# First head pair's q, k, v and the gates projected together while x arrives, from ten larger SyncE transfers

## Chip, cores and metric

The kernel runs on one core of a Trainium2 chip. The metric is device time of one execution in microseconds (us). A run gives one time per execution; one further execution is profiled, and the profile's views all come from that one.

## What is computed

Two decoder layers on x of 512 positions and width 1024, batch 1, all in fp32. Layer 0 mixes positions by forgetting attention with 16 heads, layer 1 by a gated linear recurrence; behind each mixer stands a gated MLP with a causal convolution. The part around the change is the head of layer 0:

```
h = rmsnorm(x, att_norm_g)
proj = h @ w_in                       # 1024 -> 3*1024 + 16
q, k, v, fl = split(proj, [D, 2*D, 3*D])
logf = log_sigmoid(fl + b_f)
c = cumsum(logf, axis=1)
logits = q k^T / 8 + (c_t - c_s), causal
o = softmax(logits) v ; x = x + o @ w_out
```

## The kernel before

Everything is kept transposed: the 1024 features lie on 8 blocks of 128 partitions, the 512 positions on the free axis, so that x is eight blocks of 128x512. TensorE (PE) multiplies fp32 numbers in two parts. `split` (lines 66 to 68) makes of a tile a rounded part (`..h`, a cast on ScalarE, line 67) and the rest (`..l`, a subtraction on VectorE, line 68), and `mm3` (lines 81 to 84) sums three products: weight h by x h (L82), weight h by x l (L83), weight l by x h (L84). One block of 128 outputs from 1024 inputs is therefore 24 matmuls of 128x512 in one PSUM bank.

The gain of the norm is put on x first (`Norm.block`, lines 175 to 183: `xh` on ScalarE at L180, `xl` on VectorE at L181); the factor 1/rms needs all of x, so it is applied behind the projections. `Norm.square` (lines 185 to 193) sums the squares (`nsq` on ScalarE, `nacc` on VectorE), and `Norm.finish` (lines 195 to 208) sums over partitions with a plain fp32 matmul (`nss`, L199) and makes `rstd` of it.

The start stands at lines 231 to 269. SyncE (SP) issues the gains, x block 0, and then weights and x in pieces (`pieces`, line 238): x blocks 0, 1 to 3, 4 to 7, each piece led by its part of the q and the k weights of head pair 0 (`wst`, tiles of 64, 192 and 256 KB). Per block of x, six matmuls go into the banks of q and k (`pj_q0`, `pj_k0`). Behind them come the norm, the v weights of head pair 0 as one 512 KB transfer (line 265, `pj_v0`, 24 matmuls), and the forget gates (lines 266 to 269, `pj_wf`: 24 matmuls with only 16 output rows). The attention section (lines 303 to 509) then runs as four generators that take turns: `projections` (q, k, v of the other seven head pairs, each by a 512 KB transfer through `chunk` into one of two `raw` tiles), `operands` (`qk`, `forget`, `values`: scaling by `rstd`, and for q and k small SP copies into the tiles QX, QQ, KX, KK), `maxima` (row maxima `mxp`) and `attend` (`lg`, `pv`). Results stay in `oh`, `ol` of `opool`, whose buffers x and the first weights used before.

The text gives what depends on what; the order in which each engine's instructions stand is set when the program is built, by the framework's scheduler, engine by engine, and each engine then runs its list in that order. A transposition `vT` (L351) of the v of head pair 0 is the first PE instruction that needs `rstd`.

## Time and profile before

| | us |
|---|---|
| median of 3 runs | 1275.23 (1274.2 to 1275.55) |
| profiled execution, its own time | 1275.21 |
| its span | 1273.5 |
| PE busy | 1252.6 (98%) |
| DVE busy (VectorE) | 802.7 (63%) |
| ACT busy (ScalarE) | 589.7 (46%) |
| POOL busy (GpSimd) | 44.7 (4%) |
| the chain that ended last, share of PE | 94% |

The span is the time from the first to the last instruction in the profile; the execution's own time is 1.7 us more. PE's matmuls are pipelined: a matmul's duration in a row (0.39 us) is longer than the distance from its start to the next one's start (0.23 us), so times of a row of matmuls are read from their starts. PEld is the load of the next stationary operand.

### The profile page before, as it was taken

To read this page: it belongs to the slowest core of one execution; us is meant where nothing else is said; L and a number is where in the kernel's file an instruction comes from. 1 tells how busy PE (TensorE), PEld (TensorE's weight loads), DVE (VectorE), ACT (ScalarE), POOL (GpSimd) and SP (SyncE) were. 2 spreads that over 40 slices of the span, in tenths; PEclk is the share of its full clock that TensorE was granted. 3 is DMA by queue.
4 is the path that set the end of the run, shared out by engine and by line. 5 is a ranking of instruction groups with operands and counts; after the bars stand their busy time and mean duration, and the time that the engine had idled before them with its cause. 6 is when DMAs were issued, how large, how long until landed. Compare 5 with 4: busy or idle time off the path is not lost.

```text
span 1273.5 us, 15653 instructions
## 1 busy us (share of the span) xinstructions
PE 1252.6 (98%) x5994; PEld 1039.3 (82%) x5994; DVE 802.7 (63%) x1227; ACT 589.7 (46%) x827; POOL 44.7 (4%) x120
## 2 busy tenths in 40 slices
PE   7999999999999999999999999999999999999997
PEld 5778888888888888888888988987888888888886
DVE  6767767387777777333367585566777777762233
ACT  6355556464444444222266565554544444442231
POOL 2011110000000000000010000000000000000001
PEclk9999999999999999999999999999999999999998
DMA  6544554233333333333322222222233332333321
GB/s 197 149 128 108 134 134 124 89 127 99 100 100 99 98 91 91 91 98 98 95 85 82 81 70 83 84 67 92 91 100 99 100 98 90 96 90 93 96 85 66
DMA packets 43307, 127.25 MB, mean 100 GB/s; under 512 B 5617, under 2 KB 8305, under 8 KB 43233
## 3 DMA queue, kind: packets, MB, share of 16 engines
q1 hardware_dynamic: 42592, 125.56, 32.9%
q8 instruction: 47, 0.77, 0.3%
q10 hardware_dynamic: 544, 0.52, 0.1%
q14 instruction: 28, 0.22, 0.1%
q0 software_dynamic: 96, 0.18, 0.1%
HBM read 111.43 MB, written 2.10 MB: 89 GB/s over the span
## 4 chain that ended last, share of the span: by engine, by line
PE 94%; DVE 2%; ACT 2%; DMA 1%; issue 0%; SPq 0%; POOL 0%; DVEq 0%; ACTq 0%
PE pj_up L84 13%; PE pj_up L82 13%; PE pj_up L83 13%; PE pj_dn L82 6%; PE pj_dn L84 6%; PE pj_dn L83 6%; PE i L634 1%; PE i L633 1%; PE i L631 1%; PE pj_who L83 1%; PE pj_who L84 1%; PE pj_who L82 1%; PE pj_hf L82 1%; PE pj_hf L83 1%; PE pj_hf L84 1%; PE pj_hg L84 1%
## 5 line engine op out<-in xcount | busy, mean ns | idle before, releaser
L82 PE MATMUL pj_up<-xh_f,wh_up 128*128 128x512 f32 x704 | 273.9, 389 | 0.0
L83 PE MATMUL pj_up<-xl_f,wh_up 128*128 128x512 f32 x704 | 273.9, 389 | 0.0
L84 PE MATMUL pj_up<-xh_f,wl_up 128*128 128x512 f32 x704 | 273.9, 389 | 0.0
L83 PEld LDWEIGHTS pj_up<-xl_f,wh_up 128*128 128x128 f32 x704 | 132.2, 188 | 27.6
L84 PEld LDWEIGHTS pj_up<-xh_f,wl_up 128*128 128x128 f32 x704 | 132.2, 188 | 27.4
L82 PEld LDWEIGHTS pj_up<-xh_f,wh_up 128*128 128x128 f32 x704 | 132.2, 188 | 27.3
L82 PE MATMUL pj_dn<-gh,wh_dn 128*128 128x512 f32 x330 | 130.8, 396 | 0.0
L83 PE MATMUL pj_dn<-gl,wh_dn 128*128 128x512 f32 x330 | 130.8, 396 | 0.0
L84 PE MATMUL pj_dn<-gh,wl_dn 128*128 128x512 f32 x330 | 130.8, 396 | 0.0
L67 ACT CAST wh_up<-raw_up 128x1024 fp32r<-128x1024 f32 x88 | 92.7, 1054 | 65.9 <-PE pj_up L83 50.6
L68 DVE TENSOR_TENSOR wl_up<-raw_up,wh_up 128x1024 fp32r<-128x1024 f32 x88 | 107.9, 1226 | 15.4 <-ACT wh_up L67 11.9
L68 DVE TENSOR_TENSOR wl_dn<-raw_dn,wh_dn 128x1024 fp32r<-128x1024 f32 (+1 forms) x45 | 51.1, 1136 | 98.2 <-ACT wh_dn L67 97.9
L543 DVE TENSOR_TENSOR us<-pj_up,rstd_f 128x512 f32<-128x512 f32 x88 | 60.6, 688 | 78.4 <-PE pj_up L84 78.2
L67 ACT CAST wh_dn<-raw_dn 128x1024 fp32r<-128x1024 f32 (+1 forms) x45 | 44.1, 980 | 140.4 <-PE pj_dn L83 109.1
L67 ACT CAST gh<-y 128x512 fp32r<-128x512 f32 x44 | 27.3, 621 | 115.5 <-DVE y L551 115.5
L546 ACT ACTIVATE y<-us,cv 128x512 f32<-128x512 f32 x88 | 71.7, 815 | 8.5 <-DVE us L543 7.3
L84 PEld LDWEIGHTS pj_dn<-gh,wl_dn 128*128 128x128 f32 x330 | 62.2, 188 | 15.2
L83 PEld LDWEIGHTS pj_dn<-gl,wh_dn 128*128 128x128 f32 x330 | 62.2, 188 | 15.2
L82 PEld LDWEIGHTS pj_dn<-gh,wh_dn 128*128 128x128 f32 x330 | 62.1, 188 | 15.1
L548 DVE SCALAR_TENSOR_TENSOR y<-us,cv,y 128x512 f32<-128x512 f32 x88 | 66.2, 752 | 3.0
L547 DVE SCALAR_TENSOR_TENSOR y<-us,cv,y 128x512 f32<-128x512 f32 x88 | 65.7, 746 | 0.2
L550 ACT ACTIVATE y<-y 128x512 f32<-128x512 f32 x44 | 27.8, 632 | 79.5 <-DVE y L548 79.5
(369 smaller groups left out, 2379.3 us busy)
## 6 DMA issues: line engine op xcount, KB each, us to landing
raw_up<-in_wup SPq DMA_DIRECT2D x88, 512.0 KB
raw_dn<-in_wdn SPq DMA_DIRECT2D x30, 512.0 KB
raw_dn<-in_wdn SPq DMA_DIRECT2D x15, 384.0 KB
raw_v<-in_wqkv SPq DMA_DIRECT2D x8, 512.0 KB
raw_wo<-in_wo SPq DMA_DIRECT2D x8, 512.0 KB
raw_hf<-in_wh SPq DMA_DIRECT2D x8, 512.0 KB
raw_hq<-in_wh SPq DMA_DIRECT2D x8, 512.0 KB
raw_hg<-in_wh SPq DMA_DIRECT2D x8, 512.0 KB
```

The costliest lines, as they stand in the source:

```text
L67: A.copy(dst_h, src)
L68: V.tensor_tensor(dst_l, src, dst_h.bitcast(F32), op=ALU.subtract)
L82: PE.matmul(o, wh_, xh_, start=first, stop=False)
L83: PE.matmul(o, wh_, xl_, start=False, stop=False)
L84: PE.matmul(o, wl_, xh_, start=False, stop=last)
L543: V.tensor_mul(u[:, 2:], o, rstd)
L546: A.activation(y, u[:, 2:], AF.Identity, scale=k(2), bias=k(3))
L547: V.scalar_tensor_tensor(y, u[:, 1:S + 1], k(1), y, op0=ALU.mult, op1=ALU.add)
L548: V.scalar_tensor_tensor(y, u[:, 0:S], k(0), y, op0=ALU.mult, op1=ALU.add)
L550: A.activation(ys[0], ys[0], AF.Silu)
L631: PE.matmul(o, xh[kk][:, ts_], hs, start=kk == 0 and i % 2 == 0, stop=False, skip_group_check=True)
L633: PE.matmul(o, xh[kk][:, ts_], ls, start=False, stop=False, skip_group_check=True)
```

## The change

SP loads the start in ten transfers (five of x, five of weights): x blocks 0 and 1 singly, then in pairs, and from a new input `wqkv0`, in which the host has put the q, k and v weights of head pair 0 side by side by block of x, block 0 singly, blocks 1 and 2, 3 and 4, 5 and 6 in pairs, block 7 singly. The gains go out on ScalarE's queue and the gates' weights on GpSimd's. Eight matmuls on a constant tile (`warm`) stand ahead of everything on PE. Per block of x, nine matmuls go into the banks of q, k and v; the gates' weights lie in one tile `fw` of 48 columns per block (h part in columns 0 to 15, l part in 32 to 47, zeros between), so that two matmuls per block, 16 in place of 24, give both parts, which `forget` adds (one ScalarE copy and one VectorE addition more). The squares are interleaved with the blocks, and `nss` comes behind the gates. `oh` and `ol` become four tiles of two blocks each. Line numbers of the changed kernel from here on are higher than before by 3 to 17 (`split` is still L67 and L68, `mm3` is L85 to L87, `xl` is L184, `nacc` L196, the gates' matmuls L261 and L262).

```diff
@@ -228,45 +231,54 @@
         def tmp(name, rows=P):
             return ap_.tile([rows, S], F32, tag="tmp", name=name, bufs=3)
+        norm = Norm(G_ATT, "a")
+        warm = side("warm")
+        for i in range(8):
+            PE.matmul(warm[:, :P], ones, ones, start=True, stop=True)
+        xin = [opool.tile([P, 2, S], F32, name=f"xin{j}", bufs=1, tag=f"oh{j}") for j in range(NT)]
+        fraw = ap_.tile([P, NB, HEADS], F32, name="fraw", tag="tmp", bufs=3)
+        nc.scalar.dma_start(gn, gains)
+        nc.gpsimd.dma_start(fraw, wf)
+        wst = []
+        for i, (wa, wb, xa, xb) in enumerate(((0, 1, 0, 1), (1, 3, 1, 2), (3, 5, 2, 4), (5, 7, 4, 6), (7, 8, 6, 8))):
+            nc.sync.dma_start(flat(xin[xa // 2][:, xa % 2:xa % 2 + xb - xa]), flat(xT[:, xa:xb]))
+            w = (ap_.tile([P, 1, 3, P], F32, name="wst0", tag="tmp", bufs=3) if i == 0 else
+                 opool.tile([P, 2, 3, P], F32, name=f"wst{wa}", bufs=1, tag=f"ol{i - 1}"))
+            nc.sync.dma_start(flat4(w[:, :wb - wa]), flat4(wqkv0[:, wa:wb]))
+            wst += [w[:, j] for j in range(wb - wa)]
+        xin = [xin[j // 2][:, j % 2] for j in range(NB)]
         A.preload_act_table_set("natural_log_exp_and_others")
-        norm = Norm(G_ATT, "a")
-        xin = [opool.tile([P, S], F32, name=f"xin{j}", bufs=1, tag=f"oh{j}") for j in range(NB)]
-        wst = [opool.tile([P, S], F32, name=f"wst{j}", bufs=1, tag=f"ol{j}") for j in range(6)]
-        wqk = [[wpool.tile([P, 1024], F32R, tag=t, name=f"{t}_qk{w}") for t in ("wh", "wl")] for w in range(2)]
-        pieces = ((0, 1), (1, 4), (4, 8))
-        nc.sync.dma_start(gn, gains)
-        nc.sync.dma_start(xin[0], xT[:, 0])
-        for i, (a, b) in enumerate(pieces):
-            for w in range(2):
-                nc.sync.dma_start(wst[2 * i + w][:, :(b - a) * P], flat(wqkv[w * 8][:, a:b, :]))
-            for j in range(max(a, 1), b):
-                nc.sync.dma_start(xin[j], xT[:, j])
-        oq, ok = bank("pj_q0"), bank("pj_k0")
+        fw = ap_.tile([P, NB, 48], F32R, name="fw", tag="tmp", bufs=3)
+        G.memset(fw.bitcast(F32), 0.0)
+        oq, ok, ov, of = bank("pj_q0"), bank("pj_k0"), lbank("pj_v0"), side("pj_wf")
+        def gates(j):
+            PE.matmul(of[:48], fw[:, j], norm.xh[j], start=j == 0, stop=False)
+            PE.matmul(of[:48], fw[:, j], norm.xl[j], start=False, stop=j == NB - 1)
         for j in range(NB):
-            for i, (a, b) in enumerate(pieces):
-                if j == a:
-                    for w in range(2):
-                        c = slice(a * P, b * P)
-                        split(wqk[w][0][:, c], wqk[w][1][:, c], wst[2 * i + w][:, :(b - a) * P])
+            if j % 2 == 0:
+                wh2, wl2 = (wpool.tile([P, 2, 4, P], F32R, tag=t, name=f"{t}_qkv{j}") for t in ("wh", "wl"))
+            h, l = wh2[:, j % 2], wl2[:, j % 2]
             norm.block(j, xin[j], sq=False)
-            c = slice(j * P, (j + 1) * P)
-            for o, (h, l) in zip((oq, ok), wqk):
-                mm3(o, h[:, c], l[:, c], norm.xh[j], norm.xl[j], j == 0, j == NB - 1)
+            split(h[:, :3], l[:, :3], wst[j])
+            if j == 1:
+                split(fw[:, :, 0:HEADS], fw[:, :, 32:32 + HEADS], fraw)
+            if j:
+                norm.square(j - 1, xin[j - 1])
+            for w, o in enumerate((oq, ok, ov)):
+                mm3(o, h[:, w], l[:, w], norm.xh[j], norm.xl[j], j == 0, j == NB - 1)
+            if j > 1:
+                gates(j - 2)
+        norm.square(NB - 1, xin[NB - 1])
+        gates(NB - 2)
+        gates(NB - 1)
         xh, xl = norm.xh, norm.xl
-        for j in range(NB):
-            norm.square(j, xin[j])
         rstd = norm.finish(load=None)
-        fraw = opool.tile([P, NB, HEADS], F32, name="fraw", bufs=1, tag="ol6")
-        nc.sync.dma_start(fraw, wf)
-        fwh = opool.tile([P, NB, HEADS], F32R, name="fwh", bufs=1, tag="ol7")
-        fwl = ap_.tile([P, NB, HEADS], F32R, tag="tmp", name="fwl", bufs=3)
-        ov = finish(proj(wqkv[16], xh, xl, "v0", bank=lbank))
-        split(fwh, fwl, fraw)
-        of = side("pj_wf")
-        for k in range(NB):
-            mm3(of[:HEADS], fwh[:, k], fwl[:, k], xh[k], xl[k], k == 0, k == NB - 1)
         cv = cpool.tile([P, 2, 2 * NF, 4], F32, name="cv")
         nc.gpsimd.dma_start(cv, convs)
...
@@ -303,7 +315,9 @@
         def forget():
 
             z, e = tmp("fz", HEADS), tmp("fe", HEADS)
-            V.tensor_mul(z, of[:HEADS], rstd[:HEADS])
+            A.copy(e, of[32:32 + HEADS])
+            V.tensor_tensor(z, of[:HEADS], e, op=ALU.add)
+            V.tensor_mul(z, z, rstd[:HEADS])
             V.tensor_scalar(z, z, bft, None, op0=ALU.add)
             V.scalar_tensor_tensor(e, z, -1.0, z, op0=ALU.mult, op1=ALU.max)
             A.activation(e, e, AF.Exp, scale=-1.0)
...
@@ -501,8 +515,10 @@
                 V.tensor_mul(dn, dn, rc)
                 V.scalar_tensor_tensor(rc, dn, 2.0, rc, op0=ALU.subtract, op1=ALU.mult, reverse0=True)
                 V.tensor_mul(o32, o32, rc)
-                oh[hp] = opool.tile([P, S], F32R, tag=f"oh{hp}", name=f"oh{hp}", bufs=1)
-                ol[hp] = opool.tile([P, S], F32R, tag=f"ol{hp}", name=f"ol{hp}", bufs=1)
+                if hp % 2 == 0:
+                    pair[:] = [opool.tile([P, 2, S], F32R, tag=f"{n}{hp // 2}", name=f"{n}{hp}", bufs=1)
+                               for n in ("oh", "ol")]
+                oh[hp], ol[hp] = (t[:, hp % 2] for t in pair)
                 split(oh[hp], ol[hp], o32)
                 done["out"] += 1
 
...
@@ -864,6 +880,7 @@
         "convs": np.concatenate([cw, cb[:, None]], axis=1).reshape(2, 4, 2 * NF, P).transpose(3, 0, 2, 1),
         "bf": arr(att_b_f)[0][:, None],
         "wqkv": cols(w_in[:, :3 * D]),
+        "wqkv0": np.stack([cols(w_in[:, :3 * D])[8 * w] for w in range(3)], axis=2),
         "wf": w_in[:, 3 * D:].reshape(NB, P, HEADS).transpose(1, 0, 2),
         "wo": cols(arr(att_w_out)[0]),
         "wup": np.stack([cols(w) for w in arr(ffn_w_up)]),
```

The order that comes of it, at three places. First PE, at the start of the program, before (q and k of head pair 0; `wh_qk0` and `wl_qk0` are the two parts of its q weights, `xh_a0` and `xl_a0` those of x block 0):

```order
L82 MATMUL pj_q0_117<-xh_a0_123,wh_qk0_98 128x512
L83 MATMUL pj_q0_117<-xl_a0_124,wh_qk0_98 128x512
L84 MATMUL pj_q0_117<-xh_a0_123,wl_qk0_99 128x512
L82 MATMUL pj_k0_118<-xh_a0_123,wh_qk1_100 128x512
L83 MATMUL pj_k0_118<-xl_a0_124,wh_qk1_100 128x512
L84 MATMUL pj_k0_118<-xh_a0_123,wl_qk1_101 128x512
L82 MATMUL pj_q0_117<-xh_a1_137,wh_qk0_98 128x512
L82 MATMUL pj_k0_118<-xh_a1_137,wh_qk1_100 128x512
L83 MATMUL pj_q0_117<-xl_a1_138,wh_qk0_98 128x512
```

and with the change (`warm` is the constant tile's product, `wh_qkv0` the weights of blocks 0 and 1):

```order
L239 MATMUL warm_83<-ones_73 128x128 x8
L261 MATMUL pj_wf_120<-xh_a0_123,fw_115 48x512
L85 MATMUL pj_q0_117<-xh_a0_123,wh_qkv0_121 128x512
L86 MATMUL pj_q0_117<-xl_a0_124,wh_qkv0_121 128x512
L87 MATMUL pj_q0_117<-xh_a0_123,wl_qkv0_122 128x512
L85 MATMUL pj_k0_118<-xh_a0_123,wh_qkv0_121 128x512
L86 MATMUL pj_k0_118<-xl_a0_124,wh_qkv0_121 128x512
```

A gates' matmul on x block 0, which reads the tile `fw`, now stands ahead of the first q matmul.

Second VectorE, from its first row before:

```order
L278 CAST onesr_313<-ones_73 128x128
L181 SCALAR_TENSOR_TENSOR xl_a0_124<-xin0_84,gn_67,xh_a0_123 128x512
L68 TENSOR_TENSOR wl_qk0_99<-wst0_92,wh_qk0_98 128x128
L68 TENSOR_TENSOR wl_qk1_101<-wst1_93,wh_qk1_100 128x128
L68 TENSOR_TENSOR wl_qk0_99<-wst2_94,wh_qk0_98 128x384
L68 TENSOR_TENSOR wl_qk1_101<-wst3_95,wh_qk1_100 128x384
```

and with the change, rows 4 to 15 of its list (rows 2 and 3 are `xl` of x blocks 0 and 1; the suffix of `xin` counts pairs of blocks, that of `xl` blocks):

```order
L196 TENSOR_TENSOR nacc_a_146<-nacc_a_146,nsq_a1_165 128x512
L68 TENSOR_TENSOR wl_qkv0_122<-wst1_103,wh_qkv0_121 128x384
L184 SCALAR_TENSOR_TENSOR xl_a2_160<-xin1_93,gn_67,xh_a2_159 128x512
L184 SCALAR_TENSOR_TENSOR xl_a3_180<-xin1_93,gn_67,xh_a3_179 128x512
L196 TENSOR_TENSOR nacc_a_146<-nacc_a_146,nsq_a2_185 128x512
L288 CAST identr_305<-ident_68 128x128
L196 TENSOR_TENSOR nacc_a_146<-nacc_a_146,nsq_a3_207 128x512
L184 SCALAR_TENSOR_TENSOR xl_a4_202<-xin2_94,gn_67,xh_a4_201 128x512
L184 SCALAR_TENSOR_TENSOR xl_a5_222<-xin2_94,gn_67,xh_a5_221 128x512
L68 TENSOR_TENSOR fw_115<-fraw_96,fw_115 128x8x16
L196 TENSOR_TENSOR nacc_a_146<-nacc_a_146,nsq_a4_227 128x512
L68 TENSOR_TENSOR wl_qkv0_122<-wst0_100,wh_qkv0_121 128x384
```

The part of `fw` that VectorE writes stands behind `xl` of x block 5, and the l part of block 0's weights (`wst0`) two rows later; before, the l parts of block 0's weights were rows 3 and 4.

Third SP, from its first row before:

```order
L239 DMA gn_67<-in_gains 128x64
L240 DMA xin0_84<-in_xT 128x512
L243 DMA wst0_92<-in_wqkv 128x128
L243 DMA wst1_93<-in_wqkv 128x128
L243 DMA wst2_94<-in_wqkv 128x384
L243 DMA wst3_95<-in_wqkv 128x384
L245 DMA xin1_85<-in_xT 128x512
L245 DMA xin2_86<-in_xT 128x512
```

and with the change, its ten transfers:

```order
L248 DMA xin0_92<-in_xT 128x512 x2
L251 DMA wst1_103<-in_wqkv0 128x768
L248 DMA xin1_93<-in_xT 128x1024
L251 DMA wst3_106<-in_wqkv0 128x768
L248 DMA xin2_94<-in_xT 128x1024
L251 DMA wst5_109<-in_wqkv0 128x768
L251 DMA wst0_100<-in_wqkv0 128x384
L248 DMA xin3_95<-in_xT 128x1024
L251 DMA wst7_112<-in_wqkv0 128x384
```

In the text of the change the weights of block 0 (`wst0`) are the second transfer; in SP's list they are the eighth of ten (the first row stands for two), behind six blocks of x and the weights of blocks 1 to 6. ScalarE's list agrees: its cast of `wst0` is row 16, behind `xh` of blocks 0 to 5 (rows 3 to 13) and its part of `fw` (row 14).

## Rows read from the trace of the kernel before

**Rows 1.** Whom PE waited for over the whole span: us, times, longest.

```profile
PE pj_q L82 <- ACT wh_qk L67: 5.5, 1, 5.5
PE mxp L407 <- DMA KX<-kh: 2.0, 1, 2.0
PE pj_q L82 <- ACT xh_a L180: 1.3, 1, 1.3
...
PE vT L351 <- DVE v L347: 0.7, 1, 0.7
```

**Rows 2.** Busy time by stretch: PE, PEld, DVE, ACT, POOL (instructions), PEclk, DMA, GB/s.

```profile
2.00:4.00 2.00, 0.00 (x0) 0.00 (x0) 0.00 (x0) 0.09 (x1) 1.96 (x5) 1.00 0.86 205
4.00:6.00 2.00, 0.49 (x1) 0.29 (x1) 0.69 (x2) 1.45 (x4) 2.00 (x5) 1.00 0.84 300
6.00:8.00 2.00, 2.00 (x6) 1.49 (x5) 1.19 (x5) 1.12 (x3) 1.94 (x7) 1.00 0.82 168
...
9.90:14.30 4.40, 4.38 (x10) 3.37 (x11) 4.39 (x7) 4.40 (x9) 0.00 (x0) 1.00 1.06 398
...
1000.00:1273.50 273.50, 264.07 (x1212) 218.09 (x1210) 146.76 (x191) 97.42 (x125) 3.52 (x4) 0.99 0.30 91
```

**Rows 3.** PE in order of time: start, us, instruction.

```profile
5.51 0.80 PE L82 MATMUL pj_q<-xh_a,wh_qk 128*128 128x512 f32 x1 [5.51 <-ACT wh_qk L67]
...
9.92 0.79 PE L82 MATMUL pj_q<-xh_a,wh_qk 128*128 128x512 f32 x1 [1.31 <-ACT xh_a L180]
...
13.93 0.61 PE L82 MATMUL pj_k<-xh_a,wh_qk 128*128 128x512 f32 x1
14.36 0.42 PE L83 MATMUL pj_k<-xl_a,wh_qk 128*128 128x512 f32 x1
...
28.02 0.40 PE L82 MATMUL pj_wf<-xh_a,fwh 128*16 128x512 f32 x1
...
33.52 0.39 PE L82 MATMUL pj_q<-xh_a,wh_q 128*128 128x512 f32 x1
```

**Rows 4.** SP's issues and the first use of x, in order of time.

```profile
0.82 0.39 SPq L239 DMA_DIRECT2D gn<-in_gains  x1
1.27 0.42 SPq L240 DMA_DIRECT2D xin<-in_xT  x1
...
4.55 0.72 ACT L180 ACTIVATE xh_a<-xin,gn 128x512 fp32r<-128x512 f32 x1 [2.46 <-DMA xin<-in_xT]
```

**Rows 5.** ScalarE and VectorE by group, 5 to 34 us: busy, mean ns | idle.

```profile
L181 DVE SCALAR_TENSOR_TENSOR xl_a<-xin,gn,xh_a 128x512 fp32r<-128x512 f32 x8 | 5.6, 746 | 5.4 <-ACT xh_a L180 5.4
L180 ACT ACTIVATE xh_a<-xin,gn 128x512 fp32r<-128x512 f32 x8 | 5.4, 712 | 3.8 <-DMA xin<-in_xT 3.8
L193 DVE TENSOR_TENSOR nacc_a<-nacc_a,nsq_a 128x512 f32<-128x512 f32 x7 | 4.8, 684 | 0.0
```

**Rows 6.** Weights' parts, the end of `rstd` and its first use, in order of time.

```profile
7.33 0.51 ACT L67 CAST wh_qk<-wst 128x384 fp32r<-128x384 f32 x1 [0.72 <-DMA wst<-in_wqkv]
...
7.87 0.56 DVE L68 TENSOR_TENSOR wl_qk<-wst,wh_qk 128x384 fp32r<-128x384 f32 x1 [0.67 <-ACT wh_qk L67]
...
18.17 0.28 DVE L68 TENSOR_TENSOR fwl<-fraw,fwh 128x128 fp32r<-128x128 f32 x1
...
28.28 0.69 DVE L324 TENSOR_TENSOR q<-pj_q,rstd_a 128x512 f32<-128x512 f32 x1
```

**Rows 7.** The chain that ended last, in order of time: start, us, what.

```profile
22.74 0.87 PE nss_a L199 x2
23.70 0.70 ACT rsy_a L216
24.42 0.69 DVE rsa_a L219
...
26.42 1.23 DVE wl_k L68
...
33.82 0.60 DVE fz L306
...
40.84 0.70 DVE v L347
41.68 0.63 PE vT L351 x4
```

More of the change, by code (lines that the diff above doesn't have):

```diff
@@ L35, in trunk @@
 @with_exitstack
-def trunk(ctx, tc, xT, gains, convs, bf, wqkv, wf, wo, wup, wdn, wh, wi, who, out):
+def trunk(ctx, tc, xT, gains, convs, bf, wqkv, wqkv0, wf, wo, wup, wdn, wh, wi, who, out):
     nc = tc.nc
@@ L79, in flat, with flat4 @@
         return ap.rearrange("p a b -> p (a b)")
+    def flat4(ap):
+        return ap.rearrange("p a b c -> p (a b c)")
     def mm3(o, wh_, wl_, xh_, xl_, first, last):
@@ L357, in values @@
             done["v"] += 1
-        oh, ol = [None] * 8, [None] * 8
+        oh, ol, pair = [None] * 8, [None] * 8, []
         queue = []
```

## The prediction

> **What bounds the kernel now.** I read four views. The table of waits says that PE is the bound and where it isn't fed: of the 20.9 us in which PE isn't busy (1273.5 less 1252.6), 5.5 us are the wait for the first weights, 1.3 us the wait for x block 1, 2.0 us a wait for KX in the attention, 0.7 us the wait for v at the first transposition [rows 1]. Most of the rest lies in the last stretch, 273.5 less 264.1 [rows 2]. So a change of the start is worth what it does to the moment at which PE begins without gaps, to the matmuls done from there, and to their pace. The timeline of PE gives all three: the first matmul starts at 5.51, the gapless part at 9.92, and the first matmul of q of head pair 1 at 33.52 [rows 3]. That last one is my mark: ahead of it stands everything that the change touches (q, k, v, gates, norm), behind it the same work in both kernels.
>
> **The pace.** From 9.92 the starts lie 0.43 us apart up to 13.93, which for 512 columns is 1.2 GHz, and from 14.36 on 0.23 us, which is 2.4 GHz [rows 3]; the granted clock reads 1.00 in the whole stretch [rows 2] and so doesn't show this step. PE had been idle until 5.51, then worked, idled 1.3 us, and worked on. Ten matmuls took 14.36 - 9.92 = 4.44 us; at the later pace, 24 gate matmuls in 33.52 - 28.02 = 5.50 us or 0.229 us each [rows 3], they would have taken 2.29. The slow stretch from 9.92 costs 2.15 us, and the six slow matmuls from 5.51 another 1.5.
>
> **The change, part by part.**
>
> Gates: 24 matmuls become 16 of the same 512 columns. The output rows grow from 16 to 48, but the pace of 0.229 us was already that of 512 columns with 16 rows. Saved: 8 x 0.229 = 1.8 us on PE.
>
> Joint q, k, v: 72 matmuls before and after. Worth nothing by itself; what counts is when they may start.
>
> The start. Here the change's order decides, and against its name. PE's list has a gates' matmul on x block 0 as its first instruction behind the warm-up. It reads `fw`, and VectorE writes its part of `fw` only behind `xl` of x block 5. The first q matmul further needs the weights of block 0, which SP loads eighth of ten. PE runs its list in order, so all 71 other projection matmuls are queued behind these two waits, however early x block 0 lands. I work out when x blocks 4 and 5 land. Ahead of them and with them SP loads 256 + 256 + 384 + 512 + 384 + 512 = 2304 KB, and 272 KB of gains, gates' weights and convolution weights run beside: 2.64 MB. Before, 205, 300 and 168 GB/s moved in the stretches from 2 to 8 us, 1.35 MB, and 398 GB/s from 9.9 us on [rows 2]. At that pace 2.64 MB are moved at 8 + 1.29/0.398 = 11.2 us. SP issues its first x 0.45 us earlier, since the gains no longer stand ahead [rows 4]: 10.8. From the last byte to the waiting engine I add 1.1 us: x block 0 and the gains, 0.29 MB, were moved by 3.4 us at 205 GB/s and used at 4.55 [rows 2, 4]. So 11.9. If the dip of 6 to 8 us belonged to the small weight pieces, which are gone, 1.61 MB would follow at 398 GB/s from 6 us: 6 + 4.05 - 0.45 + 1.1 = 10.7. If early issue gained nothing and 300 GB/s held later, 8 + 4.3 + 1.1 = 13.4. I take 11.4, between the first two.
>
> The Trainium skill speaks for larger pieces: "DMA: Bandwidth & Descriptors", section "Bandwidth", asks for transfers of 1 MiB for 75% of the peak, so by it 256 KB should fall well short and ten larger transfers should gain. Here 256 KB transfers of x already move in a stream at 398 GB/s [rows 2], so by the row there is nothing to gain after 10 us; by the rule alone the stream would end sooner and my sum would fall by at most the 1.2 us between 11.9 and 10.7.
>
> From the landing: ScalarE makes `xh` of block 4 (0.71), VectorE `xl` of 4 and 5 (0.75 each) [rows 5], then its part of `fw` (0.28) [rows 6]: 2.5 us. PE's first real matmul starts at 13.9, with bounds 13.2 and 15.9. VectorE's own work could not have set this: its rows ahead (six `xl`, three `nacc`, one weight part, two small ones) are some 7.4 us from about 4.8 on [rows 5, 6]. The weights of block 0 land about (384 + 192) KB / 398 GB/s = 1.5 us after x block 5, at 12.9; ScalarE reaches their cast about 14.3 and VectorE ends their l part at 15.2. The first three matmuls at the slow pace start at 13.9, 14.3 and 14.8, and the fourth, which needs that part, at 15.2: no further wait. After that ScalarE and VectorE only have casts of 0.5 us and parts of 0.56 us per block [rows 6] against nine matmuls of 2.1 us; they stay ahead.
>
> The warm-up: eight small matmuls that end long before 13.9. They are hidden under the wait and cost nothing; what they buy is nothing either if the clock is back at 1.2 GHz by then. No row shows PE falling back after a gap of some 9 us; bounds 0 and 3.7 us of slow stretch, and I take 2.15, the stretch from 9.92, the only gapless start that the trace has.
>
> The mark: 13.9 + 88 x 0.229 (72 and 16 matmuls, 20.15) + 0.87 (`nss` [rows 7]) + 2.15 = 37.1. Before: 33.52. So +3.55 us: PE starts 4.0 us after the gapless part began before (and 8.4 after its first matmul), and of this 1.8 are won back by the gates.
>
> Behind the mark. `nss` now stands directly ahead of q of head pair 1, where it stood 10 us earlier (22.74). `rstd` takes a ScalarE step of 0.70 and four VectorE steps of 0.69 in a row, with the gaps between about 3.8 us [rows 7] (a second ScalarE step runs beside the first of the four), so q of pair 0 is scaled by 4.6 us after the mark. On VectorE follow an added sum of the two gate parts (0.68), `ql` (0.68), a weight part of 1.2 us, and the old chain from `fz` at 33.82 to v at 41.54, 7.7 us [rows 7]: v is ready 14.9 us after the mark. PE's list puts the transposition behind 60 matmuls, 13.7 us after the mark. It waits 1.1 us, against 0.74 before [rows 1]: +0.35. Behind `k` of that chain the KX and KK copies queue on SP, with the maxima waiting; their distance in PE's list (11 projection rows) is that of before, so I leave them at zero. The added ScalarE copy lies under the q matmuls. The four paired `oh`, `ol` tiles cost nothing: the final projections stand as before relative to them.
>
> Sum: +3.55 + 0.35 = +3.9 us against the profiled execution's own time of 1275.21, which is the median (1275.23) within 0.02: **1279.1 us**.
>
> **The rivals.**
>
> The clock stays up. If the warm-up leaves PE at 2.4 GHz through the gap, 2.15 us go: 1276.9, not slower by what can be told (about 0.2%, 2.55 us). It decides from a slow stretch under 0.8 us. For it: no row shows a fall. Against it: PE started slow after its idle time at the start [rows 3], and this gap is longer than that one. Chance 0.12. The Trainium skill, "TensorE: Matmul & The Clock Gate", section "HAM oscillation", has a long idle gap put PE back at half rate, as in my sum; no row here shows such a gap.
>
> The blocks stream as the name says. If PE could start with block 0 at about 5.2 us, the mark would fall at 5.2 + 20.15 + 0.87 + 2.15 = 28.4, and the time at 1270. What speaks against it is the order itself: the `fw` wait is a true dependence. Chance 0.04.
>
> A later wait disappears. The 2.0 us wait for KX [rows 1] lies in head pair 2, and the change puts more rows between k of that pair and its maxima. That alone gives 1277.1, within the bound. Chance 0.10.
>
> A new wait comes. `rstd` is 3.8 us behind the mark where it was 5.2 us ahead (first used at 28.28 [rows 6]), so head pairs 0 to 2 are packed with fewer projections between; waits of 2 to 4 us on ScalarE, VectorE or the SP copies would give 1281 to 1283. Before, 2.0 us of that kind occurred. Chance 0.12.
>
> **How the numbers follow.** My forecast has 0.62. Slower by over 0.2% is forecast and new wait, 0.74; within 0.2%, the clock and the vanished wait, 0.22; faster, the stream, 0.04. For the range: an early start (13.2) with no slow stretch gives 1276.2, a late one (15.9) with the whole 3.7 us gives 1282.7; the stream lies outside, and part of the two mixed cases.
>
> **What would show it.** Right: a gap on PE from the warm-up's end to about 13.9 us, ended by VectorE's `fw`; starts 0.43 us apart for some ten matmuls; q of head pair 1 at about 37.1; a wait of about 1.1 us at the first transposition. Wrong: a first gates' matmul before 12 us, a pace of 0.23 us from its start, or waits in head pairs 0 to 2 that differ from 2.0 us by more than 1.

## The result and the profile after

The change makes the kernel slower: 1282.66 us (median of 4 runs, 1282.38 to 1283.91) against 1274.94 us, ratio 1.0061 with an interval of 1.0045 to 1.0077. The profiled execution took 1282.38 us, 7.2 us more than that of before, with a span of 1280.7; PE is busy for 1254.5 us of it. The forecast was 1279.1, in a range up to 1282.7: the sign was right, the size about half. The time lies just inside the range, by chance: that end of the range was worked out from a late start (15.9 us) and a slow stretch of 3.7 us, and neither came.

The table of waits of PE after the change answers to [rows 1]:

```profile
PE pj_wf L261 <- DVE fw L68: 9.0, 1, 9.0
PE mxp L421 <- DMA KX<-kh: 2.0, 2, 1.3
PE lg_c L460 <- ACT pt_a L463: 0.9, 2, 0.5
PE vT L365 <- DVE v L361: 0.9, 1, 0.9
PE rp L434 <- DVE rr L429: 0.4, 1, 0.4
```

The two waits of the start are gone; in their place stands one of 9.0 us, on VectorE's part of `fw`. The waits of the attention (`mxp`, `lg_c`, `rp`) are now spread over more places. The timeline of PE after the change, answering to [rows 3]:

```profile
1.21 3.78 PE L239 MATMUL warm<-ones 128*128 128x128 f32 x16 [1.21 <-POOL ones L61]
13.96 0.66 PE L261 MATMUL pj_wf<-xh_a,fw 128*48 128x512 f32 x1 [8.98 <-DVE fw L68]
19.46 0.39 PE L85 MATMUL pj_k<-xh_a,wh_qkv 128*128 128x512 f32 x1
...
42.99 0.39 PE L85 MATMUL pj_k<-xh_a,wh_k 128*128 128x512 f32 x1
...
94.10 0.67 PE L421 MATMUL mxp<-KX,QX 66*128 66x128 f32 x3 [0.75 <-DMA KX<-kh]
118.72 0.50 PE L421 MATMUL mxp<-KX,QX 66*128 66x128 f32 x2 [1.25 <-DMA KX<-kh]
...
283.57 0.39 PE L207 MATMUL nss_f<-nsh_f,onesr 128*128 128x512 f32 x1
```

and the two places in the kernel before by which I measure from here on (`nss_f`, at the end, is the norm behind the attention):

```profile
38.96 0.39 PE L82 MATMUL pj_k<-xh_a,wh_k 128*128 128x512 f32 x1
...
276.82 0.39 PE L204 MATMUL nss_f<-nsh_f,onesr 128*128 128x512 f32 x1
```

The first is k of head pair 1, 24 matmuls behind the mark of the prediction (the mark's own start is blurred here, since `nss` runs directly ahead of it). Call it M: what the start costs is how far M moves, 42.99 - 38.96 = +4.03 us. The second, N, is the norm behind the attention: 283.57 - 276.82 = +6.75 us. So 2.72 us are lost between M and N, in the attention, and the last 0.4 us behind N, which I did not follow. PE's idle time between M and N adds up to 4.0 us before and 5.6 after, so 1.6 of the 2.72 us stand in rows of waits; the other 1.1 us stand in no such row and stay open.

M has noise of its own. Four profiled kernels have the start of the kernel before, and their k of head pair 1 begins at 37.51 to 39.87 us, because the first transfers land, and PE goes from 0.43 to 0.23 us per matmul, earlier in one execution (at 12.5 us in the earliest) than in another (16.2 in the latest). Six have the start of the change (with small moves in the list), and their M lies between +3.56 and +4.35. N - M doesn't hold this noise.

The table of windows after the change (us, then busy time of PE, PEld, DVE, ACT, POOL, then the granted clock, DMA share and GB/s), beside [rows 2]:

```profile
6.00:8.00 2.00, 0.00 (x0) 0.00 (x0) 1.80 (x3) 0.86 (x2) 1.94 (x5) 1.00 0.97 344
8.00:10.00 2.00, 0.00 (x0) 0.00 (x0) 0.43 (x1) 1.19 (x2) 1.35 (x6) 0.78 1.04 416
10.00:12.00 2.00, 0.00 (x0) 0.00 (x0) 2.00 (x5) 2.00 (x5) 0.00 (x0) 0.50 1.04 410
18.00:20.00 2.00, 2.00 (x8) 1.58 (x7) 2.00 (x4) 0.92 (x2) 0.00 (x0) 0.66 0.00 0
```

The larger transfers do fill the dip of 6 to 8 us (344 GB/s in place of 168), but PE has nothing to do then. It is idle from 4.98 on; its granted clock falls to 0.50, which is 1.2 GHz, at 9.1 us and comes back at 19.3.

What ends the hole is on ScalarE and VectorE (`xh` and `xl` of x blocks 2 and 3, then of 4 and 5, then VectorE's part of `fw`):

```profile
8.81 1.33 ACT L183 ACTIVATE xh_a<-xin,gn 128x512 fp32r<-128x512 f32 x2 [1.95 <-DMA xin<-in_xT]
...
11.10 1.32 ACT L183 ACTIVATE xh_a<-xin,gn 128x512 fp32r<-128x512 f32 x2
```

```profile
9.57 1.41 DVE L184 SCALAR_TENSOR_TENSOR xl_a<-xin,gn,xh_a 128x512 fp32r<-128x512 f32 x2 [1.77 <-ACT xh_a L183]
...
12.30 1.41 DVE L184 SCALAR_TENSOR_TENSOR xl_a<-xin,gn,xh_a 128x512 fp32r<-128x512 f32 x2
13.62 0.29 DVE L68 TENSOR_TENSOR fw<-fraw,fw 128x128 fp32r<-128x128 f32 x1
```

The last wait for a transfer is that for x blocks 2 and 3, until 8.81. From there both engines work through their lists without a gap: ScalarE comes to block 4 at 11.10 and doesn't wait for it, and VectorE is busy from 9.57 until `fw` is done. In all six profiled kernels with this start and no longer warm-up the first gates' matmul starts 5.15 us behind that moment, which lies between 8.81 and 9.55 us.

### The profile page after: what moved, and what is told of

The parts are those of the page before. It is cut to its first block, busy times and chain, and to the rows that moved or that the text cites. A ratio compares the mean times of both kernels' runs of the same rounds, so it can differ in the third digit from the quotient of the medians.

```text
span 1280.7 us, 15670 instructions
## 1 busy us (share of the span) xinstructions
PE 1254.5 (98%) x6002; PEld 1042.0 (81%) x6002; DVE 803.7 (63%) x1229; ACT 591.0 (46%) x829; POOL 43.7 (3%) x122
## 4 chain that ended last, share of the span: by engine, by line
PE 93%; DVE 2%; ACT 2%; issue 1%; DMA 1%; POOL 0%; SPq 0%; DVEq 0%; ACTq 0%
PE pj_up L87 12%; PE pj_up L86 12%; PE pj_up L85 12%; PE pj_dn L85 6%; PE pj_dn L86 6%; PE pj_dn L87 6%; PE i L650 1%; PE i L649 1%; PE i L647 1%; PE pj_who L86 1%; PE pj_wo L85 1%; PE pj_wo L86 1%; PE pj_who L87 1%; PE pj_who L85 1%; PE pj_wo L87 1%; PE pj_hf L85 1%
## 5 line engine op out<-in xcount | busy, mean ns | idle before, releaser
L85 PE MATMUL pj_up<-xh_f,wh_up 128*128 128x512 f32 x704 | 273.9, 389 | 0.0
L87 PE MATMUL pj_up<-xh_f,wl_up 128*128 128x512 f32 x704 | 273.9, 389 | 0.0
L85 PEld LDWEIGHTS pj_up<-xh_f,wh_up 128*128 128x128 f32 x704 | 132.1, 188 | 27.5
L87 PEld LDWEIGHTS pj_up<-xh_f,wl_up 128*128 128x128 f32 x704 | 132.1, 188 | 27.3
L85 PE MATMUL pj_dn<-gh,wh_dn 128*128 128x512 f32 x330 | 130.8, 396 | 0.0
L87 PE MATMUL pj_dn<-gh,wl_dn 128*128 128x512 f32 x330 | 130.8, 396 | 0.0
L67 ACT CAST wh_up<-raw_up 128x1024 fp32r<-128x1024 f32 x88 | 92.7, 1054 | 65.8 <-PE pj_up L86 51.2
L68 DVE TENSOR_TENSOR wl_up<-raw_up,wh_up 128x1024 fp32r<-128x1024 f32 x88 | 107.8, 1225 | 15.3 <-ACT wh_up L67 11.6
L68 DVE TENSOR_TENSOR wl_dn<-raw_dn,wh_dn 128x1024 fp32r<-128x1024 f32 (+1 forms) x45 | 51.1, 1136 | 97.9 <-ACT wh_dn L67 97.7
L67 ACT CAST wh_dn<-raw_dn 128x1024 fp32r<-128x1024 f32 (+1 forms) x45 | 44.1, 980 | 140.3 <-PE pj_dn L86 113.2
L67 ACT CAST gh<-y 128x512 fp32r<-128x512 f32 x44 | 27.3, 620 | 115.5 <-DVE y L567 115.5
L87 PEld LDWEIGHTS pj_dn<-gh,wl_dn 128*128 128x128 f32 x330 | 62.2, 188 | 15.2
L85 PEld LDWEIGHTS pj_dn<-gh,wh_dn 128*128 128x128 f32 x330 | 62.1, 188 | 15.1
```

What stands on the lines that cost most here:

```text
L67: A.copy(dst_h, src)
L68: V.tensor_tensor(dst_l, src, dst_h.bitcast(F32), op=ALU.subtract)
L85: PE.matmul(o, wh_, xh_, start=first, stop=False)
L87: PE.matmul(o, wl_, xh_, start=False, stop=last)
```

## Experiments

Every kernel below was timed beside the kernel before on one chip. M and N are shifts in us against the kernel before, each from one profiled execution; the last column is their difference, the loss between the two (negative: a gain).

| run | median us | ratio (interval) | M | N | N - M |
|---|---|---|---|---|---|
| the change | 1282.66 | 1.0061 (1.0045 to 1.0077) | +4.03 | +6.75 | +2.72 |
| wst0_first | 1273.67 | 0.9986 (0.9977 to 0.9995) | -4.51 | -1.55 | +2.96 |
| early_nss | 1284.14 | 1.0069 (1.0056 to 1.0081) | +4.35 | +6.94 | +2.59 |
| before_late_nss | 1278.12 | 1.0023 (1.0014 to 1.0032) | -0.11 | +3.09 | +3.20 |
| long_warm | 1281.60 | 1.0049 (1.0037 to 1.0062) | +2.29 | +4.74 | +2.45 |
| early_nss_gates | 1280.41 | 1.0037 (1.0024 to 1.0050) | +3.68 | +5.72 | +2.04 |
| wst0_first_nss | 1275.62 | 1.0000 (0.9990 to 1.0010) | -5.01 | -2.20 | +2.81 |
| wst0_first_early | 1276.04 | 1.0004 (0.9995 to 1.0014) | -5.84 | +1.68 | +7.52 |
| before_copy_add | 1277.86 | 1.0019 (1.0009 to 1.0030) | -1.45 | -0.34 | +1.11 |
| two_buffers | 1280.23 | 1.0041 (1.0027 to 1.0055) | +3.83 | +4.74 | +0.91 |
| wst0_first_two_buffers | 1271.95 | 0.9974 (0.9964 to 0.9984) | -5.20 | -3.71 | +1.49 |
| before_two_buffers | 1273.42 | 0.9990 (0.9981 to 0.9998) | +0.91 | -0.53 | -1.44 |
| wst0_first_nss_two_buffers | 1269.05 | 0.9951 (0.9938 to 0.9963) | -5.56 | -6.52 | -0.96 |
| early_nss_two_buffers | 1277.50 | 1.0016 (1.0007 to 1.0026) | +3.56 | +1.63 | -1.93 |
| no_warm | 1282.83 | 1.0060 (1.0047 to 1.0073) | +3.57 | +7.62 | +4.05 |
| best_warm14 | 1269.12 | 0.9952 (0.9940 to 0.9965) | -4.67 | -6.97 | -2.30 |

In three of these profiled executions the granted clock stands at 0.50 for a while between M and N, and N - M holds what that cost: early_nss_gates (90.2 to 93.7 us), wst0_first_early (110.2 to 117.0) and no_warm (119.9 to 123.3). The change, long_warm and no_warm have the same PE list between M and N; the two without such a stretch agree within 0.3 us. Every other edit also let the scheduler pack that list anew. How far is told below by the number of its 1144 PE instructions between M and N that stand in another order.

### The start: load order and clock

**wst0_first.** `wst0` takes the second of the three buffers of one tag, behind `fraw`, whose transfer goes out on GpSimd's queue; the scheduler puts its load eighth. Why it does so no run shows; that this place in the text does it, one edit shows (dots stand for what is left out, here and below):

```diff
-        fraw = ap_.tile([P, NB, HEADS], F32, name="fraw", tag="tmp", bufs=3)
         nc.scalar.dma_start(gn, gains)
-        nc.gpsimd.dma_start(fraw, wf)
...
             wst += [w[:, j] for j in range(wb - wa)]
+        fraw = ap_.tile([P, NB, HEADS], F32, name="fraw", tag="tmp", bufs=3)
+        nc.gpsimd.dma_start(fraw, wf)
```

> The changed kernel with one edit: the tile fraw (gates' weights) and its transfer stand behind the load loop in place of ahead of it, so that wst0 gets its buffer first; in SP's list the weights of block 0 then come second of ten, and PE's list starts with q, k, v of block 0, the gates only behind block 3. Theory (the 9 us hole of the start is this load order alone): first projection matmul at 5.2 to 6.0 us, ScalarE and VectorE (1.85 and 2.0 us per block) keep up with nine matmuls of 2.06 us, q of head pair 1 (the mark) at 28.5 to 30.5 in place of 37.1; the waits behind the mark stay, because rstd still comes behind it. Time 1273.5 to 1275.5. Rival 1 (the loads or VectorE set the pace of the blocks, so that the hole is only cut into pieces): first matmul early, but waits before each block, mark at 33 or later, time 1278 or more. Rival 2 (the waits behind the mark belong to the late start): they go as well, time 1270 to 1272.

PE's timeline of this run:

```profile
5.64 0.80 PE L85 MATMUL pj_q<-xh_a,wh_qkv 128*128 128x512 f32 x1 [0.66 <-ACT wh_qkv L67]
...
10.08 0.53 PE L86 MATMUL pj_q<-xl_a,wh_qkv 128*128 128x512 f32 x1
10.44 0.39 PE L85 MATMUL pj_k<-xh_a,wh_qkv 128*128 128x512 f32 x1
```

The first projection matmul starts at 5.64 and nothing waits from there to M. The median of 1273.67 lies in the theory's span: the 9 us hole goes with this one place in the text. The edit also takes the gates' matmul away from the head of PE's list, so by itself it doesn't tell the wait for `fw` from the wait for `wst0`; long_warm, below, does. The loss behind M stays (2.96), so it doesn't belong to the hole.

**long_warm** (44 warm matmuls in place of 8) and **no_warm** (none):

> The changed kernel with 44 warm matmuls in place of 8, so that PE works through the hole up to about 13.5 us; nothing else differs. Theory (the slow stretch behind the hole is the clock that fell to 0.50 while PE was idle): matmuls 0.23 us apart from the first on at 14.0, mark 2.2 to 2.6 us earlier, time 1279.5 to 1280.5. Rival (the first projection matmuls are slow whatever ran ahead): pace 0.43 from 14.0 to 19 as in the changed kernel, time 1282 to 1283.

> The changed kernel without the eight warm matmuls. Theory (with a hole of 9 us behind it the warm-up buys nothing): first real matmul near 14.0, starts 0.43 us apart for 2.2 to 3 us of loss, time 1282.0 to 1283.5. Rival (it keeps a part of the clock through the hole): the slow stretch grows, time 1284 or more.

```profile
1.21 11.63 PE L239 MATMUL warm<-ones 128*128 128x128 f32 x88 [1.21 <-POOL ones L61]
13.84 0.50 PE L85 MATMUL pj_q<-xh_a,wh_qkv 128*128 128x512 f32 x1 [1.01 <-ACT wh_qkv L67]
14.18 0.40 PE L86 MATMUL pj_q<-xl_a,wh_qkv 128*128 128x512 f32 x1
...
15.29 0.50 PE L87 MATMUL pj_q<-xh_a,wl_qkv 128*128 128x512 f32 x1 [0.47 <-DVE wl_qkv L68]
```

With PE at work through the hole, as this timeline of long_warm shows, the next matmuls run some 0.23 us apart from the start; M comes 1.74 us earlier than in the change, 0.5 less than expected, because PE now meets the wait for the parts of block 0's weights. The median, 1281.6, is 1.1 above the expected span. So the clock does fall in the hole because PE is idle, and that is worth 1.7 us at M. One thing more did differ, against the expectation: the scheduler moved the gates' matmuls back (the first one starts at 20.87 us), so q of block 0 now leads PE's list, and it still waits until 13.84, for ScalarE's cast of `wst0`. So the late place of `wst0` is enough for the hole, without the wait for `fw`. Without any warm-up the time is that of the change: ahead of this hole the warm-up bought nothing.

### Behind M: which lateness

**early_nss** and **before_late_nss** move `nss` alone in the text, in opposite directions. The edit of early_nss (before_late_nss puts `norm.finish` behind the gates' loop and holds `nss` at that place):

```diff
-            if j:
+            if 0 < j <= 5:
                 norm.square(j - 1, xin[j - 1])
+            if j == 5:
+                for i in range(j, NB):
+                    norm.square(i, xin[i])
+                rstd = norm.finish(load=None)
             for w, o in enumerate((oq, ok, ov)):
...
-        norm.square(NB - 1, xin[NB - 1])
...
-        rstd = norm.finish(load=None)
```

> The changed kernel with one edit: the norm's sum (nss) and with it rstd stand behind the matmuls of x block 4, at row 53 of PE's list in place of row 90; start and load order are as in the changed kernel. Theory (the 3 us that came behind the mark come from rstd being ready 3.8 us behind the mark where before it was 5.2 us ahead): mark unchanged at 37 to 37.5, the waits of head pairs 0 to 4 fall back to those of before (2.9 us shown in place of 4.6), time 1279.0 to 1280.2. Rival (they come from the paired oh/ol tiles or from other rows that the scheduler moved): the waits stay, time 1282 to 1283.

> The kernel before with one edit: nss and rstd stand behind the gates' matmuls, directly ahead of q of head pair 1, as the change has them; start, loads and gates are those of before. Theory (late rstd alone makes the waits behind the mark): mark unchanged at 33.5, new waits at head pairs 0 to 4 of about 3 us in all, time 1277.5 to 1278.5. Rival (not rstd's place): 1274.7 to 1275.7.

In the kernel before, late `rstd` alone costs 1278.12 - 1275.57 = 2.55 us, as the theory had it. In the changed kernel, early `rstd` alone gains nothing: there the theory fell. So late `rstd` is enough to make the loss, and not all that makes it here. What the new order of PE's list does by itself (165 of 1144 instructions in before_late_nss, 98 in early_nss) isn't told apart from `rstd` by these two runs.

**early_nss_gates** and **before_copy_add** look at the other input of head pair 0's operands, the chain of the gates, which the change made two steps longer (a ScalarE copy, a VectorE addition). The first puts `nss` and the gates of x blocks 3 to 7 behind block 4's matmuls, the second adds two such steps to the kernel before:

```diff
-            V.tensor_mul(z, of[:HEADS], rstd[:HEADS])
+            A.copy(e, of[:HEADS])
+            V.tensor_tensor(z, of[:HEADS], e, op=ALU.max)
+            V.tensor_mul(z, z, rstd[:HEADS])
```

> The changed kernel with nss and all gates' matmuls of x blocks 3 to 7 behind the matmuls of x block 4 (nss row 53, the last gates' row 65 of PE's list, where q of head pair 1 begins at row 91); the run early_nss moved only nss and left the waits. In that run q of pair 0 was scaled early, but the cumulated gates (cc) came 1.3 us later behind the mark than before, which is the added ScalarE copy and VectorE addition, and k of pair 0 behind them. Theory (the operands of head pair 0 hang on the chain of the gates as well as on rstd, and the waits of head pairs 0 to 4 follow from how late they are): with both early, the losses behind the mark fall to those of before or lower, mark unchanged at 43.0 to 43.5 for the first k matmul, time 1278.5 to 1280. Rival (the waits come from the order in which the list was packed, whatever is ready): waits stay near 7 us of gaps, time 1282 to 1284.

> The kernel before with one edit: forget copies the gates' sums to SBUF on ScalarE and passes them through one more VectorE step (a maximum with itself, so that values stay), as the change's copy and addition do; loads, nss and gates stay. Theory (the gates' chain is on the path of head pair 0's operands): about 1.3 us later cc, k, v and vT, and as many or more waits on PE: 1276.2 to 1278. Rival (that copy and addition lie beside other work, as the prediction had it): 1274.8 to 1275.8.

The two steps cost the kernel before 1277.86 - 1274.74 = 3.1 us by the medians. By the mean granted clocks most of that is clock: two of the 12 executions have a mean granted clock of 0.998 and took 1274.66 and 1274.91 us, the other ten have 0.995 or 0.996 and took 1276.84 to 1279.90. By an estimate, the 0.002 to 0.003 that they lack are 2.6 to 3.8 us of some 1275; where in them the clock fell no trace shows. The profiled execution is the one of 1274.91: it shows a loss of 1.11 us behind M, and a start 1.45 us ahead of that of before, which is the noise of M. early_nss_gates won 2.2 us, 0.4 short of the expected span, but not by my theory: the cumulated gates (`cc`) came no earlier behind M (2.1 us, 1.9 in early_nss). What came earlier was the cast of k of head pair 1 (16.6 us behind M, 20.0 in early_nss), and that led to the runs of the next section. **wst0_first_nss** and **wst0_first_early** are the same two moves on wst0_first:

> As wst0_first_early, but only nss moved, the gates left behind the blocks. If rstd alone makes the waits: 1270 to 1271.5. If the gates' chain must be early too: between 1271.5 and 1273.5. If the packed order makes them: 1273 to 1274.5.

> Both edits at once: fraw behind the load loop (as in wst0_first) and nss and the gates behind the matmuls of x block 5 (last gates' row 63, nss row 64). Theory (start and lateness add up): the start of wst0_first (first k matmul of head pair 1 at 34.5, 4.5 us before that of the kernel before) with the waits of before: 1270 to 1271.5, which would beat both kernels. Rival (waits come from the packed order): 1273 to 1274.5 as wst0_first.

Both missed the gain: 1275.62 and 1276.04 are slower than wst0_first. Here too the clock has its part: three executions of wst0_first_nss with a mean granted clock of 0.997 or 0.998 took 1273.37 to 1273.91 us, the time of wst0_first, and the nine with 0.993 to 0.996 took 1274.75 to 1278.46. The windows of wst0_first_early show why it fell furthest:

```profile
106.00:108.00 2.00, 1.08 (x5) 0.56 (x3) 0.69 (x1) 1.51 (x3) 0.00 (x0) 1.00 0.91 313
108.00:110.00 2.00, 1.02 (x5) 0.78 (x6) 0.66 (x4) 0.00 (x0) 0.00 (x0) 1.00 1.05 228
110.00:112.00 2.00, 2.00 (x8) 1.82 (x8) 1.47 (x6) 0.00 (x0) 0.00 (x0) 0.54 0.27 56
```

A wait of 2 us for KX in head pair 3 leaves PE half idle from 106 to 110, and then the granted clock is 0.50 up to 117.

### The chain through one buffer

ScalarE's timeline of the change, the casts of k of pair 0, then q and k of pair 1:

```profile
50.62 0.62 ACT L67 CAST kh<-k 128x512 fp32r<-128x512 f32 x1 [1.16 <-DVE k L338]
...
57.48 0.62 ACT L67 CAST qh<-q 128x512 fp32r<-128x512 f32 x1 [0.64 <-DMA KK<-kh]
...
63.89 0.62 ACT L67 CAST kh<-k 128x512 fp32r<-128x512 f32 x1 [5.79 <-DMA QQ<-qh]
```

of the kernel before:

```profile
40.13 0.62 ACT L67 CAST kh<-k 128x512 fp32r<-128x512 f32 x1
...
54.66 0.62 ACT L67 CAST kh<-k 128x512 fp32r<-128x512 f32 x1 [6.08 <-DVE v L347]
```

and of early_nss:

```profile
52.67 0.62 ACT L67 CAST qh<-q 128x512 fp32r<-128x512 f32 x1 [1.52 <-DMA KK<-kh]
...
61.01 1.08 ACT L465 ACTIVATE pt_a<-lg_a 128x512 f32<-128x512 f32 x2 [7.72 <-PE lg_a L463]
62.00 1.35 ACT L67 CAST ph_a<-pt_a 128x512 fp32r<-128x512 f32 x2
63.26 0.62 ACT L67 CAST kh<-k 128x512 fp32r<-128x512 f32 x1
```

All `qh` and `kh` share one buffer (`pth`, bufs=1), all `ql` and `kl` another. So in the change each cast waits until SP's copies of the operand before have been made (the profile names those into KK and QQ), on a queue that takes 0.5 to 0.6 us to issue each copy, and the casts form a chain, ahead of the row maxima of pair 1. In the kernel before, the profile puts the release of the last cast down to VectorE's v of pair 1 (done at 54.56) and not to a copy. Against M (38.96 and 42.99) the chain begins 1.2 us behind M before and 7.6 behind it in the change, 6.5 us later, and its last cast begins 15.7 and 20.9 behind M, 5.2 later. In early_nss the first two casts are early again (k of pair 0 2.5 us behind M), but ScalarE's list there has the last one behind the exponentials of pair 0 (`pt_a`), which wait for PE, and it begins 20.0 behind M (43.31). The test gives both tags a second buffer:

```diff
-            th = ap_.tile([P, S], F32R, tag="pth", name=f"{nm}h_{hp}", bufs=1)
-            tl = ap_.tile([P, S], F32R, tag="ptl", name=f"{nm}l_{hp}", bufs=1)
+            th = ap_.tile([P, S], F32R, tag="pth", name=f"{nm}h_{hp}", bufs=2)
+            tl = ap_.tile([P, S], F32R, tag="ptl", name=f"{nm}l_{hp}", bufs=2)
```

> The changed kernel with one edit: the tiles of qh/kh and ql/kl (tags pth and ptl) get two buffers in place of one, so that the cast of one operand need not wait until SP's copies of the operand before have landed. In the traces so far the chain kh of pair 0, its SP copies, qh of pair 1, its copies, kh of pair 1 takes 13.3 us (after) and starts 6.4 us later behind the mark than before, and the loss behind the mark goes with where it ends: kh of pair 1 ends 16.3 us behind the first k matmul of head pair 1 before, 17.2 to 17.4 in early_nss_gates and before_copy_add (loss about 1 us), 20.6 to 21.6 in the changed kernel, early_nss and wst0_first (loss 2.6 to 3.0). Theory (this chain of copies through one buffer carries the late rstd on to PE): kh of pair 1 ends at 17 us or less, loss behind the mark falls by 1.5 to 2.5, time 1280.0 to 1281.3. Rival (the chain is only a symptom, PE's packed list makes the waits): kh earlier, but gaps stay near 7 us, 1282 to 1283.5.

> The edit of wst0_first and two buffers for qh/kh and ql/kl. Theory (chain of copies): 1271.0 to 1272.3, which beats both kernels; rival: 1273 to 1274 as wst0_first.

> The kernel before with two buffers for qh/kh and ql/kl alone. Theory (the chain of copies makes the 2.0 us wait for KX there too): that wait goes, 1273.0 to 1274.3. Rival (before, the chain is early enough and its wait for KX has another cause): 1274.5 to 1275.7.

> wst0_first with nss behind x block 4's matmuls and two buffers for qh/kh and ql/kl. Theory (start, rstd and chain of copies all early): the whole 4.5 to 5 us of the early start reach the end, 1270 to 1271.5, and no stretch at 1.2 GHz behind a wait of 2 us. Rival: 1273 to 1276 as wst0_first_nss.

> The changed kernel with nss behind x block 4's matmuls (as early_nss, which alone gained nothing) and two buffers for qh/kh and ql/kl (which alone gave 1280.2). Theory (late rstd and the one buffer stand in series, each hides what the other would gain): the loss behind the mark, 2.75 us in the changed kernel, 2.6 in early_nss, 0.9 in two_buffers, becomes a gain of about 1 us against the kernel before, as in wst0_first_nss_two_buffers; time 1277.3 to 1278.8. Rival (the two buffers are all of it, rstd's place counts for nothing): 1280 to 1281.

ScalarE's timeline of two_buffers:

```profile
50.41 0.62 ACT L67 CAST kh<-k 128x512 fp32r<-128x512 f32 x1 [1.16 <-DVE k L338]
53.11 0.62 ACT L67 CAST qh<-q 128x512 fp32r<-128x512 f32 x1
57.28 0.63 ACT L67 CAST kh<-k 128x512 fp32r<-128x512 f32 x1 [0.65 <-DVE v L361]
```

The waits for the copies are gone, and the chain takes 6.9 us in place of 13.3. All five medians lie in or below the theory's spans. But in before_two_buffers the time came and its reason didn't. SP's issues and PE's first row maxima of pair 2 in the kernel before:

```profile
78.47 0.33 SPq L72 DMA_DIRECT2D raw_k<-in_wqkv  x1
79.11 0.47 SPq L339 DMA_DIRECT2D KX<-kh  x1
...
83.41 0.50 PE L407 MATMUL mxp<-KX,QX 66*128 66x128 f32 x2 [1.96 <-DMA KX<-kh]
```

and in before_two_buffers:

```profile
77.01 0.39 SPq L72 DMA_DIRECT2D raw_q<-in_wqkv  x1
79.65 0.48 SPq L339 DMA_DIRECT2D KX<-kh  x1
...
82.65 0.39 PE L407 MATMUL mxp<-KX,QX 66*128 66x128 f32 x2
```

Against M the copy is issued only 0.4 us earlier. But in the kernel before it stands 0.64 us behind a weight transfer of 512 KB, and PE is released 4.30 us after its issue; the wait of wst0_first_early is of the same kind (0.43 us behind one, 4.28). With the weight transfer 2 us or more ahead, PE is released 2.3 us after the issue (the change, at 94.10 and 118.72). So the 2.0 us wait of the kernel before is in the main a copy behind a weight transfer, which the new list of SP moved apart, and not the chain.

Set in fours, the medians tell the causes in the changed kernel apart:

| start | one buffer, nss late | one buffer, nss early | two buffers, nss late | two buffers, nss early |
|---|---|---|---|---|
| the change | 1282.66 | 1284.14 | 1280.23 | 1277.50 |
| wst0_first | 1273.67 | 1275.62 | 1271.95 | 1269.05 |

With one buffer early `rstd` gains nothing in either start (+1.5, +2.0, in part clock, by the mean granted clocks of their executions), with two it gains 2.7 and 2.9. The second buffer gives 2.4 and 1.7 behind late `rstd`, 6.6 and 6.6 behind early. Late `rstd` and the single buffer stand in series: the single buffer hides all that early `rstd` would give, and late `rstd` hides most of what the buffer would. Behind M, both edits together leave no loss at all (-1.93 and -0.96; the kernel before with two buffers has -1.44). The paired `oh`, `ol` tiles and the two gate steps are in both of these kernels, so neither makes the loss by itself. What stays argued is the way between: the edits also moved PE's list (79 of 1144 instructions in two_buffers, 80 from two_buffers to early_nss_two_buffers), and how a late cast of pair 1 passes on to the waits of pairs 2 and 3 wasn't followed step by step. The waits of PE in early_nss_two_buffers:

```profile
PE pj_wf L261 <- DVE fw L68: 9.1, 1, 9.1
PE mxp L423 <- DVE mx L425: 0.9, 4, 0.2
PE vT L367 <- DVE v L363: 0.7, 1, 0.7
```

No wait for KX, `lg_c` or `rp` is left. **wst0_first_nss_two_buffers**, 1269.05 us, beats both kernels: 5.9 us below the kernel before (1274.98 beside it), 13.6 below the change, and 4.4 below before_two_buffers, which is the fair measure of the change with its load order and `nss` put right. Last, a warm-up that reaches into its first matmul (14 matmuls in place of 8):

> wst0_first_nss_two_buffers (1269.05) with 14 warm matmuls in place of 8, so that the warm-up ends at about 5.6 us, where the first projection matmul starts. In the run long_warm the warm matmuls themselves went from 0.213 to 0.111 us apart at about 4.5 us. Theory (a gap of 0.65 us behind the warm-up is what put PE back to 0.43 us per matmul until 10.3): 0.23 us from the first matmul on, up to 2.2 us less, 1266.8 to 1268. Rival (at 2.4 GHz PE overtakes ScalarE and VectorE, which need 1.85 and 2.0 us per block against 2.06, and waits per block instead): 1268.5 to 1269.5.

1269.12: no gain, so the rival's time came, though not for its reason. PE's timelines of wst0_first_nss_two_buffers and, below, of best_warm14:

```profile
1.21 3.47 PE L239 MATMUL warm<-ones 128*128 128x128 f32 x16 [1.21 <-POOL ones L61]
5.55 0.50 PE L85 MATMUL pj_q<-xh_a,wh_qkv 128*128 128x512 f32 x1 [0.87 <-ACT wh_qkv L67]
5.89 0.40 PE L85 MATMUL pj_k<-xh_a,wh_qkv 128*128 128x512 f32 x1
```

```profile
1.21 6.20 PE L239 MATMUL warm<-ones 128*128 128x128 f32 x28 [1.21 <-POOL ones L61]
7.17 0.48 PE L85 MATMUL pj_q<-xh_a,wh_qkv 128*128 128x512 f32 x1
```

Eight had already been enough in that execution (0.23 us apart behind a gap of 0.87), so that gap didn't put PE back; and 14 end so late that the first matmul starts 1.6 us later.

## Why the prediction was right or wrong

- **The hole: its cause right, its moment in part luck.** The first real matmul was forecast at 13.9 and came at 13.96, ended by `fw`, behind a load order that was read from SP's list. But the sum went by the landing of x blocks 4 and 5 (11.4) and held that "VectorE's own work could not have set this". Nobody waited for those blocks: ScalarE reached block 4 at 11.10, and it was VectorE's and ScalarE's lists behind the landing of blocks 2 and 3 (8.81) that ended the hole, 5.15 us later. Other executions of this start came at up to 14.70.
- **The slow stretch, right.** Forecast 2.15 us. The 13 matmuls from 13.96 to 19.46 take 5.50 us; at 0.229 they would take 2.98: it cost 2.5 us. That the clock falls in the gap, for which "the clock stays up" was the rival, now shows in the granted clock (0.50 from 9.1 to 19.3 us). The Trainium skill, "TensorE: Matmul & The Clock Gate", section "HAM oscillation", has idle gaps do this, and long_warm agrees.
- **The warm-up, right:** worth nothing (no_warm, 1282.83).
- **The gates and the mark, right within 0.5 us:** +4.03 at M against +3.55, where the start of the kernel before alone moves by more (37.51 to 39.87 us at M).
- **Behind the mark, wrong, and this is the step that failed.** The term was +0.35, for the transposition alone; it measured +2.72. The transposition itself came out as forecast (0.9 us, forecast 1.1). The sentence that failed is that the KX and KK copies keep their distance in PE's list, "so I leave them at zero". Equal distance in PE's list is no cover when what has to fit into it starts 6.5 us later. The later `rstd` and the two added gate steps move k of pair 0; from there the operands of two head pairs go through one buffer and SP's copies, one after the other, and with `rstd` early and a second buffer the loss is gone (-1.93). Each lateness alone costs the kernel before 2.6 (`rstd`) and 3.1 us (gate steps, most of it clock), so the prediction's "the added ScalarE copy lies under the q matmuls" was wrong as well. Nor is "behind it the same work in both kernels" the whole of it: the work is the same, but 129 of the 1144 PE instructions between M and N stand in another order.
- **The rivals.** "A new wait comes in head pairs 0 to 2" (chance 0.12) is what happened, on top of the forecast and not in its place; its waits reach to pair 3. "A later wait disappears" came and paid nothing: the wait of the kernel before, a copy behind a weight transfer, is gone, but later copies make two others, of 2.0 us together. "The blocks stream", given 0.04, is what wst0_first is, at 1273.67 and not 1270, in the main because the loss behind M stays (2.96).
- **The granted clock.** The prediction took its 1.00 up to 14.3 us for a reading; the trace has no entry there, as the last section shows.

## What to carry to other kernels

Read the load order from the queue's own list, not from the text: a tile that shares a tag with an earlier one can take its transfer far back, and PE's first instruction then waits for what stands ahead of it. When a change makes a result later, follow its users through every single-buffered tile and every queue of small copies before writing zero, and look for a large transfer directly ahead of a small copy that something waits for. Two delays in series hide each other, so neither undone alone shows its whole worth, and only the two-by-two does.

## What the runs showed that I had not expected

The granted clock of a window doesn't always tell PE's pace at the start: it reads 1.00 while matmuls start 0.43 us apart up to 10.08 in wst0_first, and 0.50 at the same pace in the change. The list of granted clocks that a trace keeps explains it. Its first entry stands at 14.39 us in the kernel before, at 10.35 in wst0_first and at 4.20 in wst0_first_nss_two_buffers; it is 1.00 each time, and at that moment the starts close up to half their distance. Ahead of the first entry nothing is recorded and the windows print 1.00, so there only the distance of the starts tells the clock. With the same eight warm matmuls PE therefore ran on at 0.43 us in one profiled execution (wst0_first) and at 0.23 in another (wst0_first_nss_two_buffers); the warm-up took 3.78 and 3.47 us. And a wait of 2 us can cost more than itself: wst0_first_early's executions with a mean granted clock of 0.993 to 0.995 took 1276.5 to 1278.9 us, those with 0.996 or 0.997 1273.7 to 1275.6.
